# Attention by groups of four heads: both score pairs first, the values one group later

## The chip, the cores and the metric

The kernel runs on one core of a Trainium2 chip. The metric is the device time of one execution in microseconds. Before the change it is 2298.22 us, the median of three runs (2294.17 to 2298.32).

## What is computed

Two decoder layers over 1024 tokens of width 1024, all in float32. The first layer mixes tokens by sparse attention, the second by a short gated convolution; a SwiGLU follows each. The change touches the attention, of which this matters:

```python
# 16 heads of 64, in 4 groups of 4 that share one key and value head; blocks of 128 queries
score  = einsum(relu(qi . ki), wi)             # the "indexer", causal
sel    = top_k(score, 256)                     # keys that a query may see
logits = q . k * 64 ** -0.5                    # -1e30 where the key isn't selected
p      = softmax(logits)
o      = p @ v
x      = x + g1 * (o @ w_out)
```

Every sub-layer's input is normed, scaled and shifted by a modulation vector, which is a product of the conditioning vector with a weight matrix (the "ada" work below).

## The kernel before

**A planner writes the order.** The program is first recorded as operations with a priority, an engine, a cost and the tiles that they read and write (`Plan.record`, `Plan.matmuls`). `Plan.drain` then simulates the engines and emits each engine's instructions in one fixed order: of what is ready on the engine that is free first, the operation with the least priority number, and among equals the one recorded first. `Plan.take` makes one exception for TensorE: if the best candidate has another array shape than the last matmul, a ready one of the same shape goes first, if its priority is within STAY = 4 us. The chip has no say: each engine runs its queue in the order emitted, and waits where an operand is late. Everything therefore shows in the profile under one line, L244, where the planner emits.

**Array shapes.** Full matmuls and transposes use the whole array. A score product uses 64 rows of it, two heads side by side (weights 64x128); a value product uses 64 columns, again two heads (weights 128x64). In the simulation a matmul of another shape than the one before costs CHANGE = 0.15 us more.

**Rings.** `Pool.tile` gives a tile with a tag one of `bufs` slots. A new tile waits for all operations on the tile that was given `bufs` tiles earlier, and for the tile before it to have been given; slots are so passed on strictly in turn.

**The attention stage** (`Attention.attend`, L1203) goes over eight blocks `b` of 128 queries; the keys seen are `wd` = 128 (b + 1). Within a block it goes over four groups `g` of four heads, and each group has two pairs `pr`. A pair goes through these steps:

- `front` (L1262): score products into a two-bank PSUM tile "L" (two of these exist), at most 512 keys at a time, so one product for blocks 0 to 3 and two for blocks 4 to 7. DVE adds the mask and takes the row maximum in one instruction (`masked`; in the profile `p<-ps_L,bias`), writing the probability tile `p`. ACT then applies the exponential in place and sums the rows (`p<-p,nm,qsc`). The ring "p" has four tiles of 1024 columns; a pair takes one of these in blocks 0 to 3 and two in blocks 4 to 7.
- `values` (L1294): TensorE transposes the probabilities, 128 columns at a time, into one of three PSUM banks ("mm" twice, "sm" once), four to a bank. ACT or DVE copies the bank to a slice "pf" (seven slots), and the value products add up in the one bank "o", a half for each pair.
- `group_end` (L1321) scales the group's sums by the reciprocal row sums, which are spread by two transposes (`rw`), and splits the result into two parts for the output product.

Before the change a pair's `front` is followed by its own `values`, and only `group_end` is put off, behind the transposes of the next group's first pair. The priority rises with each pair.

Beside it lie `ada_next` (weights `adaw` by DMA, one DVE step each, two to four a group from block 2 on) and `out_tile` (the output product of the first half, one tile a group in blocks 4 and 5). DVE and ACT also finish the key selection of the later blocks. All DMAs of the stage are issued on SP's queue. The keys lie in the "key arena", one tile of eight rows of 1024 columns: rows 4 to 7 hold the four key heads, rows 0 to 3 held the indexer's keys and queries in the stage before.

Of the kernel before, what the change touches and what calls it, by code (L numbers as in the profile page):

```python
# [50 lines left out]
class Store:  # L51


    def __init__(self, space):
        self.space, self.real, self.parts, self.ops = space, None, {}, []
        self.alloc, self.closed = None, False
# [59 lines left out]
class Pool:  # L116
# [8 lines left out]

    def tile(self, shape, dtype, name, tag=None, bufs=None):
# [13 lines left out]
        if tag is not None:  # L140
            ring = self.rings.setdefault(tag, [])
            ring.append(st)
            if len(ring) > 1:
                plan.link(ring[-2].alloc, al)
            if len(ring) > bufs:
                old = ring[-1 - bufs]
                old.closed = True
                for o in old.ops:
                    plan.link(o, al)
# [12 lines left out]
class Plan:  # L162
# [6 lines left out]
    CHANGE = 0.15  # L169
# [126 lines left out]
    def note(self, op, refs, outs):  # L296
# [3 lines left out]
        for st in op.stores:  # L300
            assert not st.closed, "a tile is used after its ring has moved on"
            st.ops.append(op)
            if st.alloc is not None:
                st.pool.pending += 1
                self.link(st.alloc, op)
# [86 lines left out]
    def drain(self, *pools):  # L392

        held = []
        while any(p.pending for p in pools) if pools else True:
# [40 lines left out]
            if e == "tensor":  # L436
                cost = cost * self.clock(t, cost) + (self.CHANGE if op.form != self.form else 0.0)
                self.form = op.form
            self.free[e] = end = t + cost
            if op.lat:  # L440
                self.dma = max(self.dma, end) + (op.lat - 1.6)
                end = self.dma + 1.6
# [5 lines left out]
            self.finish(op, end)  # L448


P = 128
T = 1024
# [343 lines left out]
class Attention:  # L796
# [406 lines left out]
    def attend(self):  # L1203
        tk, nc, plan = self.tk, self.nc, self.plan
        self.o, self.banks, tail = [], 0, None
        self.steps = [(layer, j, i, k) for layer, j in ((0, 2), (0, 3), (0, 4), (0, 5), (1, 0))
                      for i in range(NH) for k in range(KT)]
        for b in range(TB):
# [12 lines left out]
            for g in range(KVH):  # L1221
                for _ in range((0, 0, 2, 2, 4, 4, 4, 4)[b]):
                    plan.pri = t0 + (t1 - t0) * g / 4.0
                    self.ada_next()
                sums = self.at.tile([P, GRP], F32, name="sums", tag="sums", bufs=3)
                ops = None
                for pr in range(2):
                    plan.pri = t0 + (t1 - t0) * (2 * g + pr) / 8.0
                    pts = self.front(q, b, g, pr, sums)
                    if pr == 0:  # L1230
                        prev, tail = tail, None
                    ops = self.values(pts, b, g, pr, ops, prev if pr == 0 else None)
                tail = (b, g, ops, sums)
                if b in (4, 5):
                    self.out_tile(0, 4 * (b - 4) + g)
        self.group_end(*tail)
# [24 lines left out]

    def front(self, q, b, g, pr, sums):  # L1262
# [4 lines left out]
        if wd <= HW:  # L1267
            p = sp.tile([P, T], F32, name="p", tag="p", bufs=4)
            pts = [p.part_of(r)[:, r * HW:r * HW + wd] for r in range(2)]
# [609 lines left out]
```

## Time and profile before

| | us |
|---|---|
| median of three runs | 2298.22 |
| profiled execution | 2296.28 |
| its span, first to last instruction | 2294.6 |
| PE busy, of the span | 2217.9 (97%) |
| DVE busy | 1913.8 (83%) |
| ACT busy | 1123.6 (49%) |
| DMA, mean | 154 GB/s |
| granted TensorE clock, mean | 0.986 |

PE is the tensor engine, PEld its loading of weights, DVE the vector and ACT the scalar engine, SP the engine whose queue issues DMAs. Matmuls overlap in the array, so the busy time of PE counts overlapping durations once, and a full PE can still hold waits: the distance between the starts of two instructions tells what one costs. A row of a group view gives busy time, the mean of one in ns, then the idle time of the engine ahead of these instructions and what ended it. A row of the waits gives the total, the number and the longest.

### The profile page before, as it was taken

The numbers are of one execution on the slowest core, as the hardware profiler recorded it, in microseconds if no ns is written. First come the engines' busy times: TensorE is split into PE (matmuls) and PEld (weight loads), VectorE is DVE, ScalarE is ACT, GpSimd is POOL, SyncE is SP. The second block draws the span as 40 slices with busy tenths as digits, with TensorE's granted clock in tenths as the row PEclk, the third lists the DMA queues.
The fourth block names the chain that finished last, engine by engine and source line by source line (L and its number), as shares of the span: only waits on it lengthen the run. The fifth ranks groups of instructions, "written<-read, shape, count | busy, mean of one in ns | idle before, by whom it ended". The sixth has DMA issues, their size and how long they took to land.

```text
span 2294.6 us, 32635 instructions
## 1 busy us (share of the span) xinstructions
PE 2217.9 (97%) x11435; PEld 1779.9 (78%) x11435; DVE 1913.8 (83%) x3856; ACT 1123.6 (49%) x2135; POOL 4.2 (0%) x19
## 2 busy tenths in 40 slices
PE   4999999989999989999999999999999999999999
PEld 3667866766798868888888877777888788888887
DVE  7899999786689898888797998896899887767974
ACT  5487899746755323333445552224553333334444
POOL 0000000000000000000000000000000000000000
PEclk7999999999999999999999999999999999999999
DMA  9322333533345665544983354434446532339824
GB/s 308 111 56 76 100 102 102 157 118 95 112 143 147 197 199 163 188 135 161 364 314 105 97 147 124 120 101 155 128 131 194 160 120 88 124 128 383 291 88 138
DMA packets 332318, 353.74 MB, mean 154 GB/s; under 512 B 19289, under 2 KB 216954, under 8 KB 332154
## 3 DMA queue, kind: packets, MB, share of 16 engines
q1 hardware_dynamic: 331944, 351.52, 48.1%
q8 instruction: 90, 1.47, 0.3%
q14 instruction: 74, 0.61, 0.1%
q10 hardware_dynamic: 210, 0.14, 0.0%
HBM read 278.97 MB, written 68.94 MB: 152 GB/s over the span
## 4 chain that ended last, share of the span: by engine, by line
PE 66%; DVE 19%; DMA 10%; issue 3%; ACT 1%; SPq 0%; ACTq 0%; DVEq 0%
PE ps_g L244 34%; PE ps_mm L244 24%; PE ps_sm L244 5%; DVE wlo L244 3%; DVE s L244 3%; DVE u L244 3%; PE ps_L L244 3%; DMA raw<-in_conv_w_in_dram 2%; PE ps_o L244 2%; DMA ph<-in_ffn_w_down_dram 2%; DVE v L244 2%; DVE p L244 1%; DMA raw<-in_ffn_w_up_dram 1%; DMA adaw<-in_ada_w_dram 1%; DVE adacc L244 1%
## 5 line engine op out<-in xcount | busy, mean ns | idle before, releaser
L244 ACT CAST whi<-raw 128x512 fp32r<-128x512 f32 (+1 forms) x301 | 184.8, 619 | 406.9 <-PE ps_g L244 150.0
L244 PE MATMUL ps_g<-t,whi 128*128 128x512 f32 x1184 | 368.1, 392 | 2.9 <-DVE whi L244 2.9
L244 ACT CAST whi<-s 128x512 fp32r<-128x512 f32 x276 | 170.8, 620 | 339.3 <-DVE s L244 132.7
L244 PE MATMUL ps_g<-h,whi 128*128 128x512 f32 x1056 | 327.4, 391 | 0.0
L244 DVE TENSOR_TENSOR wlo<-raw,whi 128x512 fp32r<-128x512 f32 (+1 forms) x314 | 214.7, 688 | 85.4 <-ACT whi L244 84.9
L244 PEld LDWEIGHTS ps_g<-t,whi 128*128 128x128 f32 x1184 | 223.7, 189 | 50.3 <-DVE whi L244 3.8
L244 PE MATMUL ps_g<-t,wlo 128*128 128x512 f32 x592 | 233.0, 394 | 1.8 <-DVE wlo L244 1.6
L244 PEld LDWEIGHTS ps_g<-h,whi 128*128 128x128 f32 x1056 | 198.3, 188 | 41.1 <-ACT whi L244 0.2
L244 PE MATMUL ps_g<-h,wlo 128*128 128x512 f32 x528 | 206.5, 391 | 2.7 <-DVE wlo L244 2.7
L244 DVE TENSOR_TENSOR wlo<-s,whi 128x512 fp32r<-128x512 f32 x276 | 189.2, 688 | 14.4 <-ACT whi L244 13.4
L244 PE MATMUL ps_mm<-t,whi 128*128 128x512 f32 x608 | 188.5, 391 | 2.1 <-ACT whi L244 2.1
L244 PE MATMUL ps_g<-ph,whi 128*128 128x512 f32 x572 | 176.6, 389 | 0.0
L244 PEld LDWEIGHTS ps_mm<-t,whi 128*128 128x128 f32 x608 | 113.7, 188 | 26.9 <-ACT whi L244 3.6
L244 PEld LDWEIGHTS ps_g<-t,wlo 128*128 128x128 f32 x592 | 112.3, 190 | 28.4 <-DVE wlo L244 5.1
L244 PEld LDWEIGHTS ps_g<-ph,whi 128*128 128x128 f32 x572 | 107.4, 188 | 22.2
L244 ACT ACTIVATE p<-p,nm,qsc 128x128 f32<-128x128 f32 (+7 forms) x128 | 111.3, 871 | 22.5 <-DVE nm L244 20.8
L244 PE MATMUL ps_mm<-t,wlo 128*128 128x512 f32 x304 | 118.8, 391 | 0.5 <-DVE wlo L244 0.5
L244 ACT ACTIVATE junk<-sc,bs 128x896 bf16<-128x896 f32 (+3 forms) x124 | 109.7, 884 | 19.6 <-DVE bs L244 12.6
L244 PEld LDWEIGHTS ps_g<-h,wlo 128*128 128x128 f32 x528 | 99.5, 188 | 24.5 <-DVE wlo L244 3.7
L244 DVE CUSTOM_DVE_ANT_0 p<-ps_L,bias 128x512 f32<-128x512 f32 (+3 forms) x192 | 100.3, 555 | 21.6 <-PE ps_sm L244 10.1
L244 DVE TENSOR_TENSOR u<-u 128x512 f32<-128x512 f32 x170 | 114.7, 688 | 1.8 <-ACT u L244 0.8
L244 DVE SCALAR_TENSOR_TENSOR adacc<-adaw,cact,adacc 128x512 f32<-128x512 f32 x140 | 104.8, 749 | 10.1 <-DMA adaw<-in_ada_w_dram 9.6
(340 smaller groups left out, 4815.3 us busy)
## 6 DMA issues: line engine op xcount, KB each, us to landing
adaw<-in_ada_w_dram SPq DMA_DIRECT2D x160, 256.0 KB, 3.0
ph<-in_ffn_w_down_dram SPq DMA_DIRECT2D x66, 512.0 KB, 5.8
raw<-in_ffn_w_gate_dram SPq DMA_DIRECT2D x54, 512.0 KB, 4.1
raw<-in_ffn_w_up_dram SPq DMA_DIRECT2D x54, 512.0 KB, 4.3
raw<-in_conv_w_in_dram SPq DMA_DIRECT2D x34, 512.0 KB, 4.3
raw<-in_ffn_w_down_dram SPq DMA_DIRECT2D x44, 256.0 KB, 2.6
ph<-in_ffn_w_down_dram SPq DMA_DIRECT2D x44, 256.0 KB, 4.6
raw<-in_attn_w_in_dram SPq DMA_DIRECT2D x18, 512.0 KB, 3.8
```

Of the source, the lines that this page charges most:

```text
L244: f(*[a.get() if isinstance(a, Ref) else a for a in args], **{k: a.get() if isinstance(a, Ref) else a for k, a in kw.items()})
```

## The change

- `attend` runs `front` for both pairs of a group first and then `values` for the whole group before; all of it has the group's priority.
- `values` transposes and copies both pairs, then makes the value products of both, then calls `group_end` at once.
- `row` gives eight probability tiles in turn: four of the ring "p", and rows 0 to 3 of the key arena.
- A ring hands a new tile whichever slot is free first, still in the order in which tiles were asked for.
- The simulation charges a change of array shape by its two shapes, and takes a DMA to land later by its size at 450 GB/s.

```diff
@@ -52,8 +52,9 @@
 
 
     def __init__(self, space):
-        self.space, self.real, self.parts, self.ops = space, None, {}, []
-        self.alloc, self.closed = None, False
+        self.space, self.real, self.parts = space, None, {}
+        self.alloc = None
+        self.ring, self.todo, self.last = None, 0, 0.0
 
 
 class Ref:
@@ -122,6 +123,21 @@
         self.gate = Op(None, 0.0, lambda: None, 0)
         self.gate.left = 1
         self.rings, self.pending = {}, 0
+
+    class Ring:
+        def __init__(self, plan, bufs):
+            self.plan, self.slots, self.asked = plan, [0.0] * bufs, []
+
+        def grant(self):
+            while self.slots and self.asked:
+                al = self.asked.pop(0)
+                al.ready = max(al.ready, heapq.heappop(self.slots))
+                al.left -= 1
+                self.plan.settle(al)
+
+        def back(self, end):
+            heapq.heappush(self.slots, end)
+            self.grant()
 
     def tile(self, shape, dtype, name, tag=None, bufs=None):
         plan = self.plan
@@ -138,15 +154,13 @@
         st.alloc = al = Op(None, 0.0, emit, 0)
         plan.link(self.gate, al)
         if tag is not None:
-            ring = self.rings.setdefault(tag, [])
-            ring.append(st)
-            if len(ring) > 1:
-                plan.link(ring[-2].alloc, al)
-            if len(ring) > bufs:
-                old = ring[-1 - bufs]
-                old.closed = True
-                for o in old.ops:
-                    plan.link(o, al)
+            ring = self.rings.get(tag)
+            if ring is None:
+                ring = self.rings[tag] = Pool.Ring(plan, bufs)
+            st.ring = ring
+            al.left += 1
+            ring.asked.append(al)
+            ring.grant()
         plan.settle(al)
         return Ref(st, dtype, np.broadcast_to(np.int8(0), tuple(shape)))
 
@@ -166,7 +180,10 @@
     SLACK = (0.3, 0.1, 0.1, 0.1, 0.0)
     WINDOW = 3.41
     BIAS = 0.8
-    CHANGE = 0.15
+    ROWS, COLS = (64, 128), (128, 64)
+    CHANGE = {(ROWS, None): 0.285, (None, ROWS): 0.115, (None, COLS): 0.12, (COLS, None): 0.15,
+              (ROWS, COLS): 0.277, (COLS, ROWS): 0.278}
+    TRAIL = 1.0 / 450e3
     STAY = 4.0
 
     def __init__(self, nc, tc):
@@ -298,8 +315,7 @@
             self.depend(op, r, any(r is o for o in outs))
         op.stores = {id(r.store): r.store for r in refs}.values()
         for st in op.stores:
-            assert not st.closed, "a tile is used after its ring has moved on"
-            st.ops.append(op)
+            st.todo += 1
             if st.alloc is not None:
                 st.pool.pending += 1
                 self.link(st.alloc, op)
@@ -434,18 +450,23 @@
             op.emit()
             cost = op.cost
             if e == "tensor":
-                cost = cost * self.clock(t, cost) + (self.CHANGE if op.form != self.form else 0.0)
+                cost = cost * self.clock(t, cost) + self.CHANGE.get((self.form, op.form), 0.0)
                 self.form = op.form
             self.free[e] = end = t + cost
             if op.lat:
                 self.dma = max(self.dma, end) + (op.lat - 1.6)
-                end = self.dma + 1.6
+                end = self.dma + 1.6 + (op.lat - 1.6) * 380e3 * self.TRAIL
                 if e == "sync":
                     self.free[e] = max(self.free[e], self.dma - 2.5)
             for st in op.stores:
                 if st.alloc is not None:
                     st.pool.pending -= 1
             self.finish(op, end)
+            for st in op.stores:
+                st.todo -= 1
+                st.last = max(st.last, end if op.lat else end + 0.25)
+                if st.todo == 0 and st.ring is not None:
+                    st.ring.back(st.last)
 
 
 P = 128
@@ -1202,7 +1223,7 @@
 
     def attend(self):
         tk, nc, plan = self.tk, self.nc, self.plan
-        self.o, self.banks, tail = [], 0, None
+        self.o, self.banks, self.rows, tail = [], 0, 0, None
         self.steps = [(layer, j, i, k) for layer, j in ((0, 2), (0, 3), (0, 4), (0, 5), (1, 0))
                       for i in range(NH) for k in range(KT)]
         for b in range(TB):
@@ -1222,18 +1243,15 @@
                 for _ in range((0, 0, 2, 2, 4, 4, 4, 4)[b]):
                     plan.pri = t0 + (t1 - t0) * g / 4.0
                     self.ada_next()
+                plan.pri = t0 + (t1 - t0) * g / 4.0
                 sums = self.at.tile([P, GRP], F32, name="sums", tag="sums", bufs=3)
-                ops = None
-                for pr in range(2):
-                    plan.pri = t0 + (t1 - t0) * (2 * g + pr) / 8.0
-                    pts = self.front(q, b, g, pr, sums)
-                    if pr == 0:
-                        prev, tail = tail, None
-                    ops = self.values(pts, b, g, pr, ops, prev if pr == 0 else None)
-                tail = (b, g, ops, sums)
+                pts = [self.front(q, b, g, pr, sums) for pr in range(2)]
+                if tail is not None:
+                    self.values(*tail)
+                tail = (pts, b, g, sums)
                 if b in (4, 5):
                     self.out_tile(0, 4 * (b - 4) + g)
-        self.group_end(*tail)
+        self.values(*tail)
 
     def attended(self, tail):
 
@@ -1259,16 +1277,31 @@
         self.banks += 1
         return self.tk.ps("sm" if self.banks % 3 == 2 else "mm")
 
+    def row(self):
+        i, self.rows = self.rows % 8, self.rows + 1
+        if i < 4:
+            p = self.at.tile([P, T], F32, name="p", tag="p", bufs=4)
+            return p.part_of(0), p.part_of(1), p
+        i -= 4
+        keys = [[("p", i, r)] for r in range(2)]
+        if self.rows <= 8:
+            for k in keys:
+                k.extend([0] if i == 0 else [("q", half, hp, two, r) for half in range(NH)
+                                             for hp in range(IH // 2) for two in range(2)
+                                             for r in range(2)])
+        a, b = (self.karena.part_of(k)[:, i] for k in keys)
+        return a, b, self.karena.part_of(keys[0] + keys[1])[:, i]
+
     def front(self, q, b, g, pr, sums):
 
         nc, sp = self.nc, self.at
         wd = (b + 1) * P
         h0 = GRP * g + 2 * pr
         if wd <= HW:
-            p = sp.tile([P, T], F32, name="p", tag="p", bufs=4)
-            pts = [p.part_of(r)[:, r * HW:r * HW + wd] for r in range(2)]
+            p = self.row()
+            pts = [p[r][:, r * HW:r * HW + wd] for r in range(2)]
         else:
-            pts = [sp.tile([P, T], F32, name="p", tag="p", bufs=4)[:, 0:wd] for _ in range(2)]
+            pts = [self.row()[2][:, 0:wd] for _ in range(2)]
         mx = sp.tile([P, 2, 2], F32, name="mx", tag="mx", bufs=5)
         nm = sp.tile([P, 2], F32, name="nm", tag="nm", bufs=5)
         n = -(-wd // HW)
@@ -1291,32 +1324,31 @@
                                  accum_out=sums[:, 2 * pr + r:2 * pr + r + 1])
         return pts
 
-    def values(self, pts, b, g, pr, ops, tail):
-
-
+    def values(self, pts, b, g, sums):
 
         tk, nc, sp, plan = self.tk, self.nc, self.at, self.plan
-        part = []
-        for c in range(0, b + 1, 2):
-            kk = range(c, min(c + 2, b + 1))
-            n = 2 * len(kk) * P
-            ps = self.bank()
-            for i, k in enumerate(kk):
-                for r in range(2):
-                    nc.tensor.transpose(ps[:, (2 * i + r) * P:(2 * i + r + 1) * P],
-                                        pts[r][:, blk(k)], tk.ident)
-            x = sp.tile([P, HW], F32, name="pf", tag="pf", bufs=7)
-            plan.copy(x[:, 0:n], ps[:, 0:n])
-            part += [x[:, 2 * i * P:2 * (i + 1) * P] for i in range(len(kk))]
-        if tail is not None:
-            self.group_end(*tail)
-        if ops is None:
-            ops = tk.ps("o")
-        for k in range(b, -1, -1):
-            plan.matmuls([(ops[r * HD:(r + 1) * HD, pr * P:(pr + 1) * P],
-                           self.vst.part_of(k)[:, k, g * HD:(g + 1) * HD],
-                           part[k][:, blk(r)]) for r in range(2)], 1.7e-3, k == b, k == 0)
-        return ops
+        parts = []
+        for pt in pts:
+            part = []
+            for c in range(0, b + 1, 2):
+                kk = range(c, min(c + 2, b + 1))
+                n = 2 * len(kk) * P
+                ps = self.bank()
+                for i, k in enumerate(kk):
+                    for r in range(2):
+                        nc.tensor.transpose(ps[:, (2 * i + r) * P:(2 * i + r + 1) * P],
+                                            pt[r][:, blk(k)], tk.ident)
+                x = sp.tile([P, HW], F32, name="pf", tag="pf", bufs=7)
+                plan.copy(x[:, 0:n], ps[:, 0:n])
+                part += [x[:, 2 * i * P:2 * (i + 1) * P] for i in range(len(kk))]
+            parts.append(part)
+        ops = tk.ps("o")
+        for pr, part in enumerate(parts):
+            for k in range(b, -1, -1):
+                plan.matmuls([(ops[r * HD:(r + 1) * HD, pr * P:(pr + 1) * P],
+                               self.vst.part_of(k)[:, k, g * HD:(g + 1) * HD],
+                               part[k][:, blk(r)]) for r in range(2)], 1.7e-3, k == b, k == 0)
+        self.group_end(b, g, ops, sums)
 
     def group_end(self, b, g, ops, sums):
 ```

## The prediction

> **What bounds the kernel now.** I read the page first, then busy time by stretch, then PE's timeline, the waits and the groups of the attention stage.
>
> ```profile
> span 2294.6 us, 32635 instructions
> PE 2217.9 (97%) x11435; PEld 1779.9 (78%) x11435; DVE 1913.8 (83%) x3856; ACT 1123.6 (49%) x2135; POOL 4.2 (0%) x19
> ```
>
> TensorE looks full, so a saving has to come from its own time. The change rewrites the attention stage, which in the timeline runs from the first score product to the last value product:
>
> ```profile
> 304.59 0.71 PE L244 MATMUL ps_L<-karena,qst 64*128 64x128 f32 x8
> ...
> 620.93 1.97 PE L244 MATMUL ps_o<-pf,vst 128*64 128x128 f32 x32
> 622.83 0.39 PE L244 MATMUL ps_mm<-ohi,wlo 128*128 128x256 f32 x1
> 623.05 0.28 PE L244 MATMUL ps_mm<-ohi,whi 128*128 128x256 f32 x1
> 623.17 0.28 PE L244 MATMUL ps_mm<-olo,whi 128*128 128x256 f32 x1
> ```
>
> That is 318 us. By stretch (us, then busy time and count of PE, PEld, DVE, ACT, POOL, granted clock, DMA share, GB/s):
>
> ```profile
> 304.00:624.00 320.00, 302.98 (x2623) 215.36 (x2622) 259.52 (x843) 239.52 (x548) 0.00 (x0) 0.98 0.39 116
> ...
> 800.00:1000.00 200.00, 193.76 (x840) 156.15 (x839) 176.76 (x295) 60.71 (x104) 0.00 (x0) 0.98 0.57 179
> ...
> 1400.00:1600.00 200.00, 194.51 (x842) 157.89 (x841) 166.33 (x284) 58.27 (x100) 0.00 (x0) 0.99 0.41 125
> ```
> ```profile
> 305.00:320.00 15.00, 13.76 (x91) 8.33 (x88) 14.84 (x74) 14.46 (x52) 0.00 (x0) 0.77 0.37 103
> ...
> 335.00:350.00 15.00, 14.44 (x116) 8.89 (x118) 15.00 (x56) 14.72 (x42) 0.00 (x0) 1.00 0.16 47
> 350.00:365.00 15.00, 13.94 (x119) 8.68 (x117) 15.00 (x45) 14.36 (x39) 0.00 (x0) 1.00 0.31 86
> ...
> 470.00:485.00 15.00, 12.10 (x80) 8.27 (x77) 14.83 (x49) 6.42 (x13) 0.00 (x0) 0.89 0.44 143
> ...
> 590.00:605.00 15.00, 15.00 (x138) 9.69 (x139) 12.86 (x37) 11.15 (x21) 0.00 (x0) 1.00 0.23 72
> ```
>
> Two regimes: up to some 380 us DVE and ACT have no free time, because they still finish the key selection; later only PE is full. How full is seen from the starts of its runs, since durations overlap. One pair of heads of the last block, and ahead of it one product of 384 columns:
>
> ```profile
> 536.91 0.92 PE L244 MATMUL ps_L<-karena,qst 64*128 64x384 f32 x4
> 537.76 0.44 PE L244 MATMUL ps_sm<-ident,p 128*128 128x128 f32 x2
> ...
> 566.50 1.75 PE L244 MATMUL ps_o<-pf,vst 128*64 128x128 f32 x28
> 568.18 0.55 PE L244 MATMUL ps_mm<-ident,p 128*128 128x128 f32 x3
> ...
> 585.58 1.97 PE L244 MATMUL ps_o<-pf,vst 128*64 128x128 f32 x32
> 587.48 0.98 PE L244 MATMUL ps_mm<-ident,p 128*128 128x128 f32 x7
> 588.30 0.60 PE L244 MATMUL ps_sm<-ident,p 128*128 128x128 f32 x4
> 588.83 1.13 PE L244 MATMUL ps_L<-karena,qst 64*128 64x512 f32 x4
> 589.89 0.44 PE L244 MATMUL ps_mm<-ident,rw 128*128 128x128 f32 x2
> 590.16 0.27 PE L244 MATMUL ps_mm<-ident,p 128*128 128x128 f32 x1
> 590.36 1.13 PE L244 MATMUL ps_L<-karena,qst 64*128 64x512 f32 x4
> 591.42 1.97 PE L244 MATMUL ps_o<-pf,vst 128*64 128x128 f32 x32
> ```
>
> Prices from start to start: 28 value matmuls take 1.68 us and 32 take 1.90, so one is 0.055 and a run pays 0.14 besides. Transposes take some 0.11 each; the single one ahead of the last product takes 0.20, so a change of array shape out of it costs 0.09. A product takes 1.06 for 512 columns and 0.85 for 384, with whatever leaving it costs. So a change out of a transpose, full-size or value run costs about 0.095 us. Between the first and the last row above PE changes shape 253 times, 173 of them paying.
>
> ```profile
> L244 ACT ACTIVATE p<-p,nm,qsc 128x128 f32<-128x128 f32 (+7 forms) x128 | 111.3, 871 | 22.5 <-DVE nm L244 20.8 <-DVE rs L244 1.4 <-DVE bs L244 0.3
> L244 DVE CUSTOM_DVE_ANT_0 p<-ps_L,bias 128x512 f32<-128x512 f32 (+3 forms) x192 | 100.3, 555 | 21.6 <-PE ps_sm L244 10.1 <-PE ps_mm L244 7.2 <-PE ps_L L244 4.2
> L244 PE MATMUL ps_L<-karena,qst 64*128 64x512 f32 (+3 forms) x384 | 87.2, 538 | 8.2 <-DVE mx L244 8.2
> L244 PE MATMUL ps_o<-pf,vst 128*64 128x128 f32 x1152 | 77.6, 280 | 0.0
> L244 PE MATMUL ps_mm<-ident,p 128*128 128x128 f32 x368 | 63.6, 286 | 2.7 <-ACT pf L244 1.7 <-DVE on L244 0.7 <-DVE rs L244 0.2
> ...
> L244 PE MATMUL ps_sm<-ident,p 128*128 128x128 f32 x208 | 39.2, 290 | 1.4 <-DVE mod L244 0.6 <-ACT pf L244 0.4
> ```
>
> PE's own work in the stage: 1152 value matmuls at 0.055 = 63; 576 transposes of p at 0.11 = 63; 96 products, 48 of 512 columns at 1.06, 16 of 384 at 0.85, and 16 each of 256 and 128, carried on by the same step of 0.21 to 0.64 and 0.43, = 82; the other 511 of the 2623, mostly full-size ones, at the 0.12 from 623.05 to 623.17 = 61. Together 269. Changes: 173 x 0.095 = 16. So of 318 us some 33 are waits, which the busy figure of 303 hides. The same walk over the starts puts 13 of these before 400 us and 20 after, and 7 of the 16 of changes before 400 us.
>
> ```profile
> PEld ps_L L244 <- DVE mx L244: 13.1, 16, 2.7
> ...
> DVE p L244 <- PE ps_sm L244: 10.1, 5, 3.0
> ...
> PE ps_L L244 <- DVE mx L244: 8.2, 10, 2.3
> DVE p L244 <- PE ps_mm L244: 7.2, 4, 3.3
> ...
> DVE adacc L244 <- DMA adaw<-in_ada_w_dram: 6.1, 9, 1.7
> ```
>
> (Total, times, longest.) PE's largest wait is for the masked maximum that empties the score bank. And DVE's masked maximum itself waits 17.3 us, in nine pieces, for transposes: that is the ring of four probability tiles, whose next tile is free only when an older one has been transposed. The two feed each other.
>
> **The change part by part.** *Order of a group.* No matmul, copy or exponential is added or removed; products of both pairs stand ahead of the transposes and values of the group before. In the last block a pair now pays four changes (into values, out of them, twice into products), eight a group. Afterwards a group of blocks 0 to 3 needs three (products, transposes, values) and one of blocks 4 to 7 about five: its four products go through two score banks, so they fall into two runs, and the ring of seven value slices can split the values of the largest blocks. 16 x 3 + 16 x 5 = 128 instead of 173: 45 x 0.095 = 4 us. Half of it lies before 400 us, where DVE and ACT set the pace and a freer PE only waits longer; I count 2. The bounds are 0 (the planner splits the runs again) and 4.
>
> [...]
>
> *Eight probability tiles.* Four of the new eight are rows of the key arena that held the index keys and queries; those are last used in the projection stage, long before 304 us, so the first use waits for nothing. The transposes are now a group behind the products, so exponentials (0.87 us on the mean) have the whole of the former group's PE work, about 12 us in the last block, to hide in. What goes is the 17.3 us of DVE's waits, and with it what PE loses to late maxima. Of the 20 us of PE waits after 400 us I take half, 10 us. The bounds are 0 and 20: what makes the rest is DVE and ACT being late with other work (at 470 to 485 us DVE is busy 14.83 of 15 with selection while PE loses 3), and that a deeper ring doesn't cure. Before 400 us I count nothing, for DVE's and ACT's work is the same; 2 either way.
>
> *Moved steps.* Transposes, their copies, the value products and the group's end move behind the next group's products. They issue no DMA, so nothing passes SP's queue or POOL's. The copies now stand behind the next exponentials on ACT at equal priority; a copy that waits there holds one of three transpose banks, and PE then takes products. The eighth slice of blocks 6 and 7 waits for the first pair's values; behind it stand only copies of the same group. At the end of the stage a whole group's values, 32 transposes and 64 value matmuls (7 us), stand after the last product instead of a pair's; PE is busy with them, so I price this at nothing, and at 1.5 us if copies can't follow.
>
> *The planner's rules.* Costs by kind of change alter the order only in the index and attention stages. A tile may now take any free slot of its ring, and a DMA is taken to land later, by 1.17 us for 512 KB and 0.58 for 256 KB. Formerly the plan had 1.38 + 1.6 = 3.0 us and 0.69 + 1.6 = 2.3 us from issue on a free queue; measured are
>
> ```profile
> adaw<-in_ada_w_dram SPq DMA_DIRECT2D x160, 256.0 KB, 3.0
> ...
> raw<-in_ffn_w_gate_dram SPq DMA_DIRECT2D x54, 512.0 KB, 4.1
> ```
>
> so the new 2.9 and 4.1 are nearer, and fewer DVE steps should be queued ahead of their data; the 6.1 us of DVE waits for adaw are part of the waits counted above. In the other stages PE's order is nearly the order of the program. Their visible idle time is 6.2 us in the stretch from 800 us and 5.5 in that from 1400. A new order can give such a piece back or open one: 0, with 6 either way.
>
> *Sum*, against the profiled execution of 2296.3 us (span 2294.6 and 1.7 around it): 2 + 10 = 12 less, 2284.3. The median of the runs, 2298.2, lies 1.9 above that execution, so the forecast is 2286.
>
> **The rivals.** *A, nearly all waits go.* Changes 4, waits 20, elsewhere 2: 26 less, 2272. For it: the 17.3 us of DVE waits are due to the ring alone. Against: the last block has almost no waits now (a pair there takes 5.84 us, 1.90 + 13 x 0.11 + 2 x 1.06 + 0.3 being 5.75).
>
> *B, nothing measurable.* The waits after 400 us come from DVE and ACT being late against the plan, and the queues still stand in a fixed order: changes give 2, waits 0 to 2, so 2294 to 2298. For it: 470 to 485 us. Against: the waits of DVE for transposes.
>
> *C, slower: the score banks.* There are two; in blocks 4 to 7 a group asks for four products in a row, and the third needs the first's bank, emptied by two maxima of about 0.69 us. If the plan puts them as close as their priority allows and DVE is later than planned, PE stands, with everything behind it in its queue. A hit is now 8.2 / 10 = 0.82 us. With both later products of all 16 groups hit, 32 x 0.82 = 26 us against 8 now: 18 more, less 4: 2312. It decides from about 15 extra hits on. For it: PE's largest wait is this one. Against: transposes of the former group are always ready to stand between, and the maxima no longer wait for tiles.
>
> *D, the clock.* 32 transposes of 0.11 us are 3.5 us; if half of such a run fell under a halved clock in each of the eight groups of blocks 6 and 7, each would take 1.75 us more: 8 x 1.75 = 14, which eats the gain: 2300. The rows speak against it: from 590 to 605 us, a third of it transposes, the clock is 1.00; it fell at 0.77 and 0.89, where PE had gaps. [...]
>
> *E, the other stages.* The new slot and landing rules cost 6 to 20 us there, by opening more pieces like that of 6.2 us: 2292 to 2306 with the gain.
>
> **How the numbers follow.** Forecast 0.48 (2278 to 2292), A 0.14, B 0.13, C 0.15, D 0.03, E 0.07. About 0.2%, 4.6 us, is what a measurement of this kernel can tell. Faster: the forecast, A and 0.02 of E, 0.64. Same: B, 0.02 of D and 0.02 of E, 0.17. Slower: C, 0.01 of D and 0.03 of E, 0.19. The range takes in A with 4 us to spare and leaves out most of C: 2268 to 2303.
>
> **What would show it.** DVE's waits for transposes near 0 (now 17.3); PE's waits for the maximum at or below 8.2; changes of shape down from 253 to some 190; the stage shorter by 8 to 16 us, nearly all after 400 us; runs of more than 16 transposes with the clock at 1.00. I am wrong if the waits for the maximum grow (C), if the stage keeps its 318 us with DVE's waits gone (B), or if the time moves outside of it (E).

## The result, and the profile after

The changed kernel takes 2282.95 us (median of four runs, 2280.44 to 2284.48) beside 2298.27 for the kernel before (four runs, 2294.17 to 2300.30): a ratio of 0.9938 [0.9924, 0.9952], or 15.3 us less. The forecast was 2286. The profiled run took 2280.44. From the page after:

```profile
span 2278.4 us, 32567 instructions
PE 2206.2 (97%) x11435; PEld 1778.6 (78%) x11435; DVE 1918.6 (84%) x3863; ACT 1119.9 (49%) x2128; POOL 5.6 (0%) x19
```

The work is the same, and PE is as "full" as before (97% of the span in both). PE's timeline after has the landmarks: the first score product, the last value products, and the first product of the feed-forward (h), ahead of which the output products end.

```profile
296.57 0.71 PE L261 MATMUL ps_L<-karena,qst 64*128 64x128 f32 x8
...
599.99 1.97 PE L261 MATMUL ps_o<-pf,vst 128*64 128x128 f32 x32
...
655.40 0.63 PE L261 MATMUL ps_g<-h,whi 128*128 128x512 f32 x2
```

And the last one before:

```profile
668.91 0.63 PE L244 MATMUL ps_g<-h,whi 128*128 128x512 f32 x2
```

Between the first score product and the last value product lie 318.0 us before and 305.1 after, which is within the shortening of 8 to 16 us that was forecast. But it isn't the gain: the span fell by 16.2. Busy time by stretch, cut at the last value matmul of block 3 and of block 7, first before, then after (columns as in the prediction):

```profile
304.60:388.20 83.60, 79.79 (x657) 50.29 (x658) 81.64 (x305) 79.87 (x230) 0.00 (x0) 0.96 0.36 99
388.20:622.60 234.40, 221.19 (x1954) 163.38 (x1952) 176.86 (x538) 158.49 (x317) 0.00 (x0) 0.99 0.40 122
```
```profile
296.60:391.70 95.10, 88.80 (x693) 55.61 (x692) 90.49 (x338) 89.70 (x249) 0.00 (x0) 0.91 0.33 96
391.70:601.70 210.00, 207.31 (x1914) 158.00 (x1908) 171.39 (x516) 152.55 (x301) 0.00 (x0) 1.00 0.38 117
...
400.00:600.00 200.00, 197.31 (x1820) 150.13 (x1818) 164.95 (x491) 145.04 (x286) 0.00 (x0) 1.00 0.38 117
```

So the difference falls into five pieces: 8.0 us less ahead of the first score product; 11.5 more in the small blocks (the clock there is 0.91 for 0.96; a group's lag of the values also puts some of block 4's products into this stretch); 24.4 less in blocks 4 to 7; 7.4 more between the last values and h (53.7 for 46.3); 2.6 less in all the rest. They add up to 16.1. The waits of the stage after:

```profile
PEld ps_L L261 <- DVE mx L261: 10.3, 22, 1.5
DVE adacc L261 <- DMA adaw<-in_ada_w_dram: 10.5, 9, 2.7
DVE karena L261 <- PE ps_L L261: 4.7, 6, 1.4
PE ps_L L261 <- DVE mx L261: 4.4, 8, 1.1
PE ps_g L261 <- DVE u L261: 3.8, 1, 3.8
DVE p L261 <- PE ps_L L261: 1.6, 4, 0.9
```

DVE's 17.3 us of waits for transposes are gone (it now waits for score products alone), and PE's for the maximum fell from 8.2 to 4.4. PE's wait for u is new. One group of block 7, in PE's timeline after:

```profile
570.48 1.99 PE L261 MATMUL ps_L<-karena,qst 64*128 64x512 f32 x8
572.40 0.77 PE L261 MATMUL ps_mm<-ident,karena 128*128 128x128 f32 x5
573.00 0.60 PE L261 MATMUL ps_sm<-ident,karena 128*128 128x128 f32 x4
573.53 1.13 PE L261 MATMUL ps_L<-karena,qst 64*128 64x512 f32 x4
```

Two products of 512 columns in one run (x8) take 1.92 us, 570.48 to 572.40; the two single ones in the prediction took 1.06 each. So joining two saves 0.20 us, which no step of the prediction had. Changes of array shape in the stage fall by 24, not by the some 60 of the forecast (253 to some 190).

### The profile page after: what moved, and what is told of

It is laid out like the page before. It is cut to its first block, busy times and chain, and to the rows that moved or that the text cites. A ratio compares the mean times of both kernels' runs of the same rounds, so it can differ in the third digit from the quotient of the medians.

```text
span 2278.4 us, 32567 instructions
## 1 busy us (share of the span) xinstructions
PE 2206.2 (97%) x11435; PEld 1778.6 (78%) x11435; DVE 1918.6 (84%) x3863; ACT 1119.9 (49%) x2128; POOL 5.6 (0%) x19
## 4 chain that ended last, share of the span: by engine, by line
PE 58%; DVE 4%; DMA 1%; issue 0%; ACT 0%; ACTq 0%; SPq 0%; DVEq 0%
PE ps_g L261 40%; PE ps_mm L261 16%; PE ps_sm L261 3%; DVE u L261 1%; DVE wlo L261 1%; DVE v L261 1%; DVE s L261 1%; DMA adaw<-in_ada_w_dram 0%; DVE xr L261 0%; DMA raw<-in_ffn_w_up_dram 0%; DMA raw<-in_ffn_w_gate_dram 0%; DMA raw<-in_conv_w_in_dram 0%; DVE cv L261 0%; DVE adacc L261 0%; DVE mod L261 0%
## 5 line engine op out<-in xcount | busy, mean ns | idle before, releaser
L261 PE MATMUL ps_g<-t,whi 128*128 128x512 f32 x1184 | 365.7, 390 | 5.1 <-ACT whi L261 2.8
L261 ACT CAST whi<-raw 128x512 fp32r<-128x512 f32 (+1 forms) x297 | 182.4, 619 | 373.6 <-PE ps_g L261 154.9
L261 ACT CAST whi<-s 128x512 fp32r<-128x512 f32 x276 | 170.9, 621 | 356.8 <-DVE s L261 193.4
L261 PE MATMUL ps_g<-h,whi 128*128 128x512 f32 x1056 | 327.0, 391 | 1.3 <-ACT whi L261 1.3
L261 DVE TENSOR_TENSOR wlo<-raw,whi 128x512 fp32r<-128x512 f32 (+1 forms) x314 | 215.2, 688 | 78.3 <-ACT whi L261 77.9
L261 PEld LDWEIGHTS ps_g<-t,whi 128*128 128x128 f32 x1184 | 221.7, 188 | 53.0 <-ACT whi L261 4.5
L261 PE MATMUL ps_g<-t,wlo 128*128 128x512 f32 x592 | 231.1, 391 | 2.3 <-DVE wlo L261 2.1
L261 PEld LDWEIGHTS ps_g<-h,whi 128*128 128x128 f32 x1056 | 197.5, 188 | 43.3 <-ACT whi L261 3.0
L261 PE MATMUL ps_g<-h,wlo 128*128 128x512 f32 x528 | 205.8, 390 | 0.6 <-DVE wlo L261 0.6
L261 DVE TENSOR_TENSOR wlo<-s,whi 128x512 fp32r<-128x512 f32 x276 | 188.4, 690 | 15.6 <-ACT whi L261 15.2
L261 PE MATMUL ps_mm<-t,whi 128*128 128x512 f32 x608 | 188.7, 392 | 4.0 <-ACT whi L261 4.0
L261 PE MATMUL ps_g<-ph,whi 128*128 128x512 f32 x572 | 177.5, 389 | 0.0
L261 PEld LDWEIGHTS ps_mm<-t,whi 128*128 128x128 f32 x608 | 114.7, 189 | 28.5 <-ACT whi L261 4.9
L261 PEld LDWEIGHTS ps_g<-t,wlo 128*128 128x128 f32 x592 | 111.2, 188 | 28.0 <-DVE wlo L261 5.2
L261 PEld LDWEIGHTS ps_g<-ph,whi 128*128 128x128 f32 x572 | 107.5, 188 | 22.2
L261 PE MATMUL ps_mm<-t,wlo 128*128 128x512 f32 x304 | 119.7, 394 | 3.2 <-DVE wlo L261 3.2
L261 DVE TENSOR_TENSOR u<-u 128x512 f32<-128x512 f32 x170 | 115.0, 690 | 7.0 <-ACT u L261 5.5
L261 DVE SCALAR_TENSOR_TENSOR adacc<-adaw,cact,adacc 128x512 f32<-128x512 f32 x140 | 104.9, 749 | 17.8 <-DMA adaw<-in_ada_w_dram 17.5
L261 PEld LDWEIGHTS ps_g<-h,wlo 128*128 128x128 f32 x528 | 99.2, 188 | 21.5 <-DVE wlo L261 1.0
L261 ACT ACTIVATE junk<-sc,bs 128x384 bf16<-128x384 f32 (+3 forms) x124 | 109.5, 883 | 12.5 <-DVE bs L261 8.0
L261 PE MATMUL ps_g<-ph,wlo 128*128 128x512 f32 x286 | 111.3, 389 | 0.0
L261 PE MATMUL ps_mm<-hlo,whi 128*128 128x512 f32 (+2 forms) x240 | 92.1, 384 | 4.1 <-DVE hlo L261 4.1
```

The costliest lines, as they stand in the source:

```text
L261: f(*[a.get() if isinstance(a, Ref) else a for a in args], **{k: a.get() if isinstance(a, Ref) else a for k, a in kw.items()})
```

## The experiments

Two theories were set against each other first: that the gain is that of the attention's order and tiles, or that of the planner's rules. The table has every kernel: ratio to the kernel before, the start of the first score product, the stretches as above (small blocks; blocks 4 to 7; from there to h; from h to the last PE instruction), and the time that the trace shows the granted clock at 0.5 between the 300th and 345th us, all of the profiled run, in us. The stretches are those of one execution each, which lies up to 5.1 us off its kernel's median (e1: 2292.79 beside 2297.89), so differences between them needn't add up to differences between medians. The ratios are to the kernel before as it ran beside each kernel (medians 2298.27 to 2300.33).

| kernel | order, tiles | median, ratio [95%] | first | 0–3 | 4–7 | to h | rest | half clock |
|---|---|---|---|---|---|---|---|---|
| before | pairs, 4 | 2298.27 | 304.6 | 83.6 | 234.4 | 46.3 | 1620.3 | 6.8 |
| after | groups, 8 | 2282.95, 0.9938 [0.9924, 0.9952] | 296.6 | 95.1 | 210.0 | 53.7 | 1617.7 | 17.1 |
| e1 | groups, 8 | 2297.89, 0.9989 [0.9980, 0.9999] | 304.3 | 95.4 | 216.9 | 51.2 | 1617.7 | 20.5 |
| e2 | pairs, 4 | 2291.82, 0.9961 [0.9946, 0.9976] | 296.6 | 89.7 | 232.4 | 46.3 | 1619.4 | 3.4 |
| e3 | groups, 4 | 2281.33, 0.9915 [0.9900, 0.9930] | 296.6 | 91.6 | 218.2 | 46.0 | 1622.0 | 3.4 |
| e4 | both, 8 | 2289.59, 0.9948 [0.9932, 0.9963] | 296.6 | 92.9 | 214.0 | 52.9 | 1621.1 | 13.7 |
| e5 | groups, 8 | 2281.78, 0.9927 [0.9909, 0.9945] | 295.8 | 94.0 | 213.0 | 52.9 | 1617.3 | 17.1 |
| e6 | groups, 8 | 2297.08, 0.9993 [0.9982, 1.0005] | 303.2 | 99.3 | 217.7 | 53.6 | 1611.7 | 20.5 |
| e7 | pairs, 4 | 2296.58, 0.9989 [0.9978, 0.9999] | 303.5 | 88.6 | 231.9 | 46.3 | 1622.2 | 10.2 |
| e8 | pairs, 8 | 2294.59, 0.9981 [0.9971, 0.9991] | 296.6 | 94.1 | 225.9 | 54.2 | 1615.7 | 20.5 |
| r9 | pairs, 4 | 2296.84, 0.9983 [0.9971, 0.9995] | 296.6 | 89.5 | 227.7 | 46.2 | 1631.1 | 10.2 |
| r10 | groups, 4 | 2293.00, 0.9978 [0.9967, 0.9989] | 302.2 | 94.3 | 219.8 | 45.9 | 1622.7 | 6.8 |
| r11 | groups, 4 | 2287.06, 0.9950 [0.9932, 0.9969] | 301.9 | 92.9 | 216.3 | 45.9 | 1622.8 | 6.8 |
| r12 | pairs, 4 | 2298.98, 1.0001 [0.9987, 1.0016] | 308.9 | 86.6 | 234.4 | 46.3 | 1614.1 | 0.0 |

**e1: the attention alone.** The kernel before with the new order and the eight tiles, and the planner as it was. A pair's value products are recorded right behind its own transposes, because by the old ring rule a group's eight slices don't go through seven slots. In `values`, against the kernel after:

```diff
-        parts = []
-        for pt in pts:
+        ops = None
+        for pr, pt in enumerate(pts):
```

> The kernel before with the new order of attention and the eight tiles alone, under the old planner rules (the old ring rule needs the value products of a pair recorded right behind its transposes; nothing else differs). Against before, the changed kernel reaches the first score product 8.0 us earlier, takes 11.5 us longer for blocks 0 to 3, 24.4 us less for blocks 4 to 7, and 7.4 us more up to the first feed-forward product. Theory 1 (the depth of the attention's pipeline gives the gain inside of the stage): first score product at 304.6 as before, blocks 4 to 7 shorter by 20 to 25 us, in all 2286 to 2294. Theory 2 (the planner's rules give it): blocks 4 to 7 stay within 5 us of the 234.4 of before, in all 2294 to 2304.

It gained 2.4 us, at the edge of what can be told from none: blocks 4 to 7 are 17.5 us shorter, and the small blocks and the way to h give back 11.8 and 4.9.

**e2: the rules alone.** After, with `attend`, `front` and `values` as before.

```diff
-                pts = [self.front(q, b, g, pr, sums) for pr in range(2)]
...
+                for pr in range(2):
+                    plan.pri = t0 + (t1 - t0) * (2 * g + pr) / 8.0
+                    pts = self.front(q, b, g, pr, sums)
...
+                    ops = self.values(pts, b, g, pr, ops, prev if pr == 0 else None)
```

> The new planner rules (rings, costs of changes, landing of DMAs) with the attention as before: pair by pair and four tiles. Theory 1: first score product near 296.6, blocks 4 to 7 near the 234.4 us of before, in all 2287 to 2293. Theory 2: 2280 to 2286, with blocks 4 to 7 near 210 us.

8.5 us less than the kernel before beside it (2300.33). The first product comes 8.0 us earlier, the end of block 3 only 1.9: up to there DVE and ACT are nearly full (81.64 and 79.87 of 83.60 us in the row of before). Neither theory holds alone: e1 and e2 add up to 10.9 of 15.3. Of its waits, for comparison with e3:

```profile
DVE p L261 <- PE ps_L L261: 8.5, 8, 2.6
DVE p L261 <- PE ps_sm L261: 6.8, 3, 2.6
DVE p L261 <- PE ps_mm L261: 4.6, 2, 2.9
PE ps_L L261 <- DVE mx L261: 3.9, 9, 0.8
PEld ps_mm L261 <- ACT pf L261: 13.7, 21, 2.1
PEld ps_sm L261 <- ACT pf L261: 11.9, 15, 1.8
PEld ps_mm L261 <- ACT p L261: 9.3, 13, 2.0
```

**e3: groups with four tiles.** After, with every tile of `row` from the ring.

```diff
-        i, self.rows = self.rows % 8, self.rows + 1
...
+        p = self.at.tile([P, T], F32, name="p", tag="p", bufs=4)
+        return p.part_of(0), p.part_of(1), p
```

> The changed kernel with four probability tiles instead of eight. A group of blocks 4 to 7 fills all four, so the next group's maxima have to wait for this group's transposes. Theory 1 with the tiles as its main part: DVE's waits for transposes come back above the 17.3 us of before, blocks 4 to 7 take 234 us or more, in all 2300 to 2330. Theory 1 with the order as its main part: blocks 4 to 7 stay near 210 us, in all 2280 to 2288. Theory 2: 2280 to 2288 as well, but then the run with the rules alone has the gain too.

At least as fast as the change: its four runs lie from 2280.19 to 2281.68. Blocks 4 to 7 take 218.2 us. Its stretches, then its waits:

```profile
296.60:388.20 91.60, 82.88 (x689) 52.99 (x688) 88.09 (x334) 88.81 (x245) 0.00 (x0) 0.98 0.35 99
388.20:606.40 218.20, 207.13 (x1927) 162.15 (x1925) 172.14 (x517) 155.02 (x309) 0.00 (x0) 0.99 0.42 129
```
```profile
DVE p L261 <- PE ps_mm L261: 4.8, 3, 2.8
PEld ps_sm L261 <- ACT pf L261: 4.6, 13, 0.7
PE ps_L L261 <- DVE mx L261: 4.4, 7, 1.6
PEld ps_mm L261 <- ACT pf L261: 4.0, 11, 0.8
PEld ps_mm L261 <- ACT p L261: 2.4, 5, 0.7
DVE p L261 <- PE ps_L L261: 0.9, 1, 0.9
DVE p L261 <- PE ps_sm L261: 0.4, 1, 0.4
```

PE's waits for the maximum are at 4.4, as in the change, but they are at 3.9 in e2 already: the order of groups is not what brought them down from 8.2. It did take DVE's waits for transposes from 11.4 (e2) to 5.2, and all of DVE's idle time ahead of its maxima from 19.9 to 6.1 us. PE's weight loads for ps_mm and ps_sm wait 8.6 us for copies, 25.6 in e2, and those for ps_mm 2.4 us for exponentials, 9.3 in e2.

**e4: pairs in blocks 0 to 3, groups from block 4.** After, with the order of before in the small blocks, to see if the order there costs the clock.

```diff
+                if b < 4:
...
+                        ops = self.values_pair(self.front(q, b, g, pr, sums), b, g, pr, ops,
+                                               prev if pr == 0 else None)
```

> The changed kernel, but blocks 0 to 3 pair by pair as before, groups from block 4 on. In the changed kernel the granted clock is at half for 17 us from 300.6 on (6.8 us before), and blocks 0 to 3 take 11.5 us longer. If the deeper order in the small blocks is what opens these gaps, blocks 0 to 3 go back to about 84 us from the first score product and the whole comes to 2270 to 2277. If the loss has another cause (the plan's order ahead of the stage, DVE and ACT being full), it stays at 2280 to 2288.

The half clock stays (13.7 us), and the small blocks take 92.9, so the order there isn't what brings it. The whole, 2289.59, is slower than either alternative said; why wasn't found.

**e8: pairs with eight tiles.** The fourth corner: e2 with `row`.

```diff
-            p = sp.tile([P, T], F32, name="p", tag="p", bufs=4)
+            p = self.row()
```

> The new planner rules, attention pair by pair as before, but eight probability tiles. Groups gave 2281.3 with four tiles and 2283.0 with eight, pairs 2291.8 with four. If the prediction's mechanism (DVE's maxima wait for tiles, and PE with them) is worth its 10 us, this run comes to 2280 to 2286. If the tiles are worth nothing, DVE's waits for transposes go to near 0 and the whole stays at 2287 to 2295.

Eight tiles cost 2.8 us here by the medians, and 1.6 from e3 to after; the kernels of each pair ran beside different runs of the kernel before, and the intervals of the ratios overlap a little in both pairs. The stretches say how. In blocks 4 to 7 eight tiles do gain, 6.5 us (232.4 to 225.9) and 8.2 (218.2 to 210.0). In the small blocks they lose 4.4 and 3.5, and on the way to h 7.9 and 7.7. DVE's idle time ahead of its maxima isn't less than with four tiles, 20.8 us for 19.9 in e2; it now ends with score products instead of transposes:

```profile
DVE karena L261 <- PE ps_L L261: 17.8, 12, 2.9
DVE p L261 <- PE ps_L L261: 3.0, 4, 1.5
```

The first loss goes with the clock. First the trace after, with the 3.41 us ahead of the fall (as long as e3's low stretch) and the 17.07 us at 0.50; then e3, with its 3.41 us at 0.50 and what follows:

```profile
297.19:300.60 3.41, 2.53 (x21) 1.61 (x19) 3.41 (x26) 3.38 (x10) 0.00 (x0) 1.00 0.13 46
300.60:317.67 17.07, 15.37 (x70) 8.64 (x70) 16.95 (x76) 14.14 (x53) 0.00 (x0) 0.50 0.36 98
```
```profile
302.60:306.01 3.41, 3.41 (x21) 2.29 (x19) 3.41 (x17) 3.41 (x15) 0.00 (x0) 0.50 0.42 135
306.01:325.00 18.99, 17.23 (x142) 10.57 (x142) 18.99 (x84) 18.64 (x62) 0.00 (x0) 1.00 0.42 113
```

All six kernels with eight tiles have 13.7 to 20.5 us of it, all eight with four tiles 0 to 10.2. It is not the whole of the loss: one more product of block 4, 1.06 us, lies ahead of the cut with eight tiles, and r10 takes 94.3 us with 6.8 at half clock. The second loss splits the same way, without overlap: 51.2 to 54.2 us to h with eight tiles, 45.9 to 46.3 with four. Its cause is in the queues. SP's, after and in e3, reloads the residual stream (xr) at the end of the stage:

```profile
598.30 9.20 SPq L261 DMA_DIRECT2D xr<-xs  x16
```
```profile
592.67 9.29 SPq L261 DMA_DIRECT2D xr<-xs  x16
```

and PE's show what it comes right behind: after, the last transposes out of the arena; in e3, the last score products from it.

```profile
597.74 0.49 PE L261 MATMUL ps_mm<-ident,karena 128*128 128x128 f32 x3
```
```profile
590.65 1.99 PE L261 MATMUL ps_L<-karena,qst 64*128 64x512 f32 x8
```

With probabilities in the arena, it is held by the last group's transposes, and the reload starts 3.4 us ahead of the last value matmul instead of 13.7. In all six kernels with eight tiles it starts 2.9 to 4.5 us ahead, in all eight with four tiles 10.1 to 13.8. ACT's queue after then shows the wait, which reaches PE, by way of DVE, as the 3.8 us for u that end at 615.9; from 614.6 on the clock is at 0.5 for 6.83 us:

```profile
607.81 3.99 ACT L261 ACTIVATE u<-xr 128x512 f32<-128x512 f32 x6 [4.54 <-DMA xr<-xs]
```

3.8, and some 2.4 of the 5.5 us at half clock behind the wait (full-size products of 256 columns start 0.213 us apart there, and 0.120 ahead of it and from 621.5 on), make 6.2 of the 7.7 us; eleven matmuls more than in e3 lie behind the last value product, at 0.12 us some 1.3. All six kernels with eight tiles have this wait of PE for u (3.3 to 5.0 us), none with four. A version that keeps the last groups out of the arena wasn't run.

**e5: one price for a change of shape.** After, with the old CHANGE.

```diff
+    CHANGE = 0.15
...
+                cost = cost * self.clock(t, cost) + (self.CHANGE if op.form != self.form else 0.0)
```

> The changed kernel with the old single cost of 0.15 us for a change of shape in the plan. If the ring rule alone brings the stage forward, the first score product stays at 295 to 299; if the costs by kind do, it goes back to 303 to 306. In the stage itself the costs decide how runs are cut: if they matter there, the changes of shape go up from 230 to 245 or more, 2284 to 2290 in all; if not, 2279 to 2286.

The prices by kind gave nothing; with the single price there are even 19 changes of shape fewer than in the change.

**e6: no later landing.** After, without the new term.

```diff
-                end = self.dma + 1.6 + (op.lat - 1.6) * 380e3 * self.TRAIL
+                end = self.dma + 1.6
```

> The changed kernel without the later landing of DMAs in the plan. If the landing rule matters as the prediction has it, DVE's waits for adaw and the waits for weights in the later stages grow and the whole comes to 2286 to 2295, or, if it brings the stage forward, the first score product goes back to 303 to 306. If it doesn't matter, 2279 to 2286 with the first score product at 295 to 299.

The whole gain is gone, and with it the early first product (303.2). That seemed to make the landing rule the cause, which the next runs test.

**e7: the ring rule alone** on the kernel before: `Pool.Ring` and what feeds it.

```diff
-            if len(ring) > bufs:
-                old = ring[-1 - bufs]
...
+            st.ring = ring
+            al.left += 1
+            ring.asked.append(al)
+            ring.grant()
```

> The kernel before with the new ring rule alone (a tile takes any free slot); costs, landing times and attention as before. The three new rules together bring the first score product from 304.6 to 296.6 us. If the ring rule does it, the first score product comes at 295 to 299 and the whole at 2287 to 2295; if one of the other rules does, it stays at 303 to 306 and the whole at 2295 to 2303.

2.9 us less than the kernel before beside it (2299.45), at the edge of what can be told from none.

**r9: the landing rule alone** on the kernel before.

```diff
+    TRAIL = 1.0 / 450e3
...
-                end = self.dma + 1.6
+                end = self.dma + 1.6 + (op.lat - 1.6) * 380e3 * self.TRAIL
```

> The kernel before with the later landing of DMAs in the plan as its only change. Theory 3, formed after the changed kernel without this rule fell back to 2297: the landing rule carries most of the gain, and the order of groups adds to it only where the rule is there. Then the first score product comes at 295 to 299 and the whole at 2288 to 2294, as with all three rules. Against it (the rules act only together, or by chance): first score product 302 to 306, 2294 to 2302.

It brings the first product to 296.6, as in the change, yet only 2.7 us in all (2299.51 beside it): behind h its profiled execution takes 10.8 more, a difference that r12 comes back to.

**r10, r11: neighbours of e3.** r10 gives DVE and ACT a slack of 0.11 us for 0.1 in the plan; r11 lets DMAs land by 300 GB/s, later still.

```diff
-    SLACK = (0.3, 0.1, 0.1, 0.1, 0.0)
+    SLACK = (0.3, 0.11, 0.11, 0.1, 0.0)
```
```diff
-    TRAIL = 1.0 / 450e3
+    TRAIL = 1.0 / 300e3
```

> The changed kernel with four tiles, with the same slack of 0.11 us. If the gain is the rules' and the order's own, 2278 to 2286 with the first score product within 2 us of 296.6; if it is chance, it can lose 5 to 15 us.

> The changed kernel with four tiles, with DMAs taken to land later still, by size at 300 GB/s instead of 450 (1.75 us for 512 KB instead of 1.17). If the rule helps because it fits the measured landing, more of it loses something: 2282 to 2290. If it helps because any reserve does, it gains again: 2274 to 2281. If the order is chance, anything from 2276 to 2296.

A hundredth of a microsecond in the plan takes the ratio from 0.9915 to 0.9978 (11.7 us between the medians), and a landing that is later still takes it to 0.9950. Both lose the early first product (302.2 and 301.9) and keep the gain in blocks 4 to 7. The place is in the projections, from 175 to 200 us; e3, then r10:

```profile
175.00:200.00 25.00, 24.55 (x126) 20.60 (x125) 24.93 (x69) 17.14 (x33) 0.32 (x1) 1.00 0.42 106
```
```profile
175.00:200.00 25.00, 22.33 (x94) 18.26 (x93) 23.95 (x74) 14.52 (x28) 0.29 (x1) 0.86 0.39 106
```

PE works on 126 matmuls or 94. The changed kernel has the first picture (126, 24.59 us busy, clock 1.00), the kernel before the second (94, 22.05, 0.88).

**r12: the same slack on the kernel before.** The edit is the first of the two above.

> The kernel before with the plan's slack for a wait between engines at 0.11 us instead of 0.10 on DVE and ACT: no rule, no step changed, but another order. It shows how far the time moves by the order alone. If the gains are the rules' own, 2294 to 2302 and the first score product within 2 us of 304.6; if the plan's order is a matter of chance on this scale, it can move by 5 to 15 us.

No change in all, with the first product 4.3 us later and the rest shorter. The traces tell what an order drawn anew does ahead of the stage and what it doesn't do behind it.

- Ahead of the stage PE's matmuls stand in one and the same order in after, e2, e3, e4 and e8, and all five start it at 296.6; so e2 and e3, and e8 and after, enter the stage alike. Over all kernels there are nine orders, and the first product comes between 295.8 and 308.9. Three of them have it early (that of after, and those of e5 and r9), all with the landing rule at 450 GB/s and a slack of 0.10. The four orders without the rule have it late, and so do r10 and r11 with it. So the rule brings the early product only in some plans; whether by its fit or by the order that happens to come out isn't shown, and which detail of the order decides was not found.
- Behind h the 1611.7 to 1631.1 us are not a matter of PE's order alone: e6 and e7 have the same one there, and take 1611.7 and 1622.2 us; e3 and after have the same one, too, with 1622.0 and 1617.7. Single executions can't price the rest to better than that.

## Why the forecast held, and where its steps failed

The sum came close because of errors that cancel; that is luck. Where PE's waits went is seen from a walk over its starts: of each distance to the next start, what is over the most frequent one for a matmul of that shape, with or without a change behind it. What the half clock loses is among these waits (us, last two columns: paying changes, one fewer than by the prediction's count, and runs of products, both up to h):

| kernel | 0–3 | 4–7 | to h | all | paying changes | runs of products |
|---|---|---|---|---|---|---|
| before | 12.9 | 25.3 | 0.3 | 38.4 | 172 | 80 |
| e2, pairs, 4 tiles | 19.5 | 23.9 | 0.3 | 43.7 | 168 | 78 |
| e3, groups, 4 | 17.9 | 22.2 | 0.3 | 40.3 | 122 | 59 |
| e8, pairs, 8 | 21.6 | 18.9 | 8.1 | 48.6 | 174 | 82 |
| after, groups, 8 | 19.5 | 10.7 | 6.7 | 36.9 | 156 | 72 |

In blocks 4 to 7 more waits went than the 10 us forecast, and most came back ahead of them and behind.

**Order of a group, counted at 2: mis-sized.** With equal rules the stage to h shortens by 12.6 us with four tiles (e2 to e3) and 15.4 with eight (e8 to after). With four tiles, paying changes fall from 168 to 122: 46 x 0.095 = 4.4, the upper bound of the step. Runs of products fall from 78 to 59: 19 joined at 0.20 make 3.8, which I had left inside the price of a product. The other 4.4 are left over; the walk finds 3.4 of waits in them. With eight tiles paying changes are 156 and not 128, and most of the 15.4 is waits (48.6 to 36.9).

**Eight tiles, counted at 10: right in its place, given back beside it.** After some 390 us they gain 6.5 to 8.2: PE's waits there fall by 5.0 with pairs and by 11.5 with groups, of which 24 more paying changes and 15 more runs of products take back 5.3. "Before 400 us I count nothing" failed: the small blocks take 3.5 to 4.4 more, 1.1 of it a product that moved ahead, the rest together with a longer half clock. And the step asked only whether the first use of the arena's rows waits, not what waits for the last: 7.7 to 7.9 us on the way to h. Together +3.0 (e3 to after) and +5.8 (e2 to e8) in place of -10. The mechanism was only half right. "What goes is the 17.3 us of DVE's waits" holds for what they wait for: with pairs, DVE idles as long ahead of its maxima with eight tiles as with four (20.8 and 19.9 us). It is the order of groups that ends this, with four tiles too (6.1).

**"Moved steps issue no DMA, so nothing passes SP's queue"** is true and missed the point: the moved transposes release the storage that a DMA on SP's queue waits for.

**The planner's rules, 0 with 6 either way.** 8.0 us came ahead of the first score product, and 8.5 in all with the rules alone, outside these bounds; the small blocks take most of the 8.0 back with pairs (e2). The reason given, fewer DVE waits for adaw in the attention stage, isn't where this came from: with the rules alone they fell only from 6.1 to 4.5, and in the change they are 10.5; the 8.0 us are won in the projections.

**The rivals.** B: 15.3 us is past the 4.6 that a measurement can tell. C: PE's waits for the maximum fell, from 8.2 us to 4.4. D: the clock is 1.00 from 400 to 600 us, with runs of 20 and 32 transposes; in the longer one, from 584.49 to 588.76 us, PE does nothing else, and the clock is 1.00 then and in the 3.41 us behind, which speaks against D. Where it fell at the start of the stage, PE had been busy for 2.53 of the 3.41 us ahead (after) and 2.39 (e3). E: time did move outside the stage, to the good side here. A's waits went from blocks 4 to 7 for the most part (25.3 to 10.7) but not from the whole (38.4 to 36.9).

What is settled: the order of groups, in blocks 4 to 7, in all kernels that have it (210 to 220 us there, 226 to 234 with pairs), and both costs of the eight tiles as to their place; for the second the traces show the chain. That the eight tiles bring the longer half clock rests on the split of 14 kernels, one execution of each; how they do is not shown. What the change is worth under a planner that draws another order can't be told to better than some 10 us: e6 has all of its attention, and its ratio is 0.9993 [0.9982, 1.0005].

## What to carry to other kernels

When storage is borrowed, look at who waits for its last use, not only at what its first use waits for. Count what a run saves inside its own instructions, too, before a regrouping is priced by its changes of shape. When an engine's wait vanishes from the list, add up its idle time over everything it waits for: the wait may only have changed its name (e8). Where a planner draws the whole order, measure a neutral neighbour of each version (a slack of 0.11 for 0.1) before a gain is put down to a rule; groups with four tiles, e3, is the version to build on here.

## What the runs showed of the chip

At the start of the stage the granted clock was at 0.5 for 3.41 us (e3), 6.83 (before), 13.65 (the second time in e8), 17.07 (after) and 20.48 (e6): one, two, four, five and six times 3.41. In the 3.41 us ahead of the fall PE was busy for 2.53 us (after) and 2.39 (e3). In e3 it was busy for all of the next 3.41, and the clock was at 1.00 behind them; after, it was busy for all of those from 304.01 us on as well, and the clock stayed at 0.5. With nothing on PE but 32 transposes (after, 584.49 to 588.76 us, PE busy for 3.99 of 4.27) the clock was at 1.00. Two single products of 512 columns took 2 x 1.06 us (before), two in one run 1.92 (after): joining two runs of 64-row products saved 0.20 us within them, beside the 0.095 estimated for leaving another shape.
